# Transposing cross-attention probabilities and half of a merged sum on VectorE instead of TensorE, in a three-branch decoder layer

## The chip, the cores and the metric

The kernel runs on one core of a Trainium2 chip. The metric is the device time of one execution in microseconds (us). Times of a profiled execution are counted from the start of its span, which is the time from its first to its last instruction.

## The reference

One pre-norm layer on 256 tokens of 1024 channels, everything in float32. The input projection feeds three branches, whose outputs are projected, gated, summed and projected once more:

```python
h = rms_norm(x, norm_g)
(qa, ka, va, ga, ub, vb, gb, qc, gc, ma, mb, mc) = split_cols(h @ w_in, IN_SPLITS)
out_a = moba_attention(rope(qa), rope(ka), va) * silu(ga)      # 6 heads x 128, causal over 256 tokens
out_b = gmlp_spatial_gate(ub, vb, ...) * silu(gb)              # 6 groups x 128 channels
mk, mv = split(rms_norm(mem, mem_norm_g) @ w_mem_kv, 2)        # 256 memory tokens
p = softmax(qc @ mk.T * 128 ** -0.5)                           # 4 heads x 128, 256 x 256 each
out_c = (p @ mv) * silu(gc)
y = sigmoid(ma) * (out_a @ w_a) + sigmoid(mb) * (out_b @ w_b) + sigmoid(mc) * (out_c @ w_c)
return rms_norm(x + y @ w_out, final_norm_g)
```

## The kernel before

All weights stream once from HBM through SyncE's DMA queue, in pieces of 1 MB into a ring of three buffers (`raw`). A piece holds two **chunks** of 128 x 1024 numbers. There are 106 chunks, here counted from 0: the input projection is chunks 0 to 81 (the memory's values are 50 to 53), the branch projections are 82 to 89 for the first 512 output channels (half 0) and 90 to 97 for the others (half 1), and the output projection is 98 to 105. Within a half the order is branch a (three chunks), b (three), c (two).

Each product is made in three passes of a rounded format (fp32r): a number is split into `hi`, its rounded copy, and `lo`, the rest, and TensorE adds hi x hi, hi x lo and lo x hi. For a chunk of weights ScalarE makes `hi` (`split_hi`, L179) and then VectorE makes `lo` (`split_lo`, L183). Four chunks have room for the split, and the split of chunk c + 3 is put out while chunk c is multiplied (`LEAD` = 3, `SPL` = 4). A chunk with tokens in the stationary operand takes 12 matmuls of 512 columns (L329 to L331), and those with features there take eight of 512 and eight of 256 columns (L420).

All other work (rope, softmax, transposes, gates) is cut into units with a set cost, and a small planner (`Units`) puts them between the chunks: it keeps a clock for each engine and puts a unit out once its inputs are ready by that clock, or once it is due. What comes out is a fixed order on each engine; every engine works strictly in its order.

The places the change touches:

- For a cross head, `c_scores`, `c_max`, `softmax_exp` and `softmax_norm` give the probabilities `p` (tokens on partitions). `c_pT` turns them with four TensorE transposes of 128 x 128 against an identity (`transpose4`, L549) into a PSUM bank, ScalarE copies the rounded part (`pth`, L717), VectorE takes the rest (`ptl`, L337), and `c_pv` multiplies with the values.
- At the end of a half, the last of six gated sums (L855, L857) leaves y with tokens on partitions in the tile `sig[half]`. `y_units` turns it, in two units of four TensorE transposes each, and splits it (L192, L193) for the output projection: half 0 is needed from chunk 98 on, half 1 from chunk 102 on.
- `rms_bcast` (L277) spreads the row scales of x and of the memory over all partitions with two float32 matmuls of a matrix of ones and a diagonal matrix (`dg`, L271).
- `xk`, the token-major x, is loaded once at the start (L229), squared for the first norm, and kept in its slot (`xr`) to the end, where it is the residual.

Of the kernel before, what the change touches and what calls it, by code (L numbers as in the profile page):

```python
# [24 lines left out]
F32 = mybir.dt.float32  # L25
F32R = mybir.dt.float32r
BF16 = mybir.dt.bfloat16
AF = mybir.ActivationFunctionType
OP = mybir.AluOpType
# [3 lines left out]
D = 1024  # L33
S = 256
KD = D // 128
HA, GB, HC = 6, 6, 4
# [28 lines left out]
PE, DVE, ACT, POOL = range(4)  # L65
# [59 lines left out]
def tile_hybrid_layer(ctx: ExitStack, tc: tile.TileContext, xw, memT, mem, x, fin_g, ln_g, w, w_sp, b_sp, rope, out):  # L125
    nc = tc.nc
    ctx.enter_context(tc.manual_schedule())
    const = ctx.enter_context(tc.tile_pool(name="const", bufs=1))
    act = ctx.enter_context(tc.tile_pool(name="act", bufs=1))
    wts = ctx.enter_context(tc.tile_pool(name="wts", bufs=1))  # L130
    work = ctx.enter_context(tc.tile_pool(name="work", bufs=2))
    psum = ctx.enter_context(tc.tile_pool(name="psum", bufs=1, space=PSUM))

    V = {}

    def slot_tile(name, shape, tag, dt=F32):
        V[name] = act.tile(shape, dt, name=name, tag=tag)
        return V[name]

    def pair(name, tag, n):  # L140

        t = slot_tile(name, [128, n, 2, S], tag, F32R)
        V[name + "h"], V[name + "l"] = t[:, :, 0, :], t[:, :, 1, :]
        return V[name + "h"], V[name + "l"]

    def bank():
        return psum.tile([128, 512], F32, name="aux", tag="aux", bufs=4)
# [4 lines left out]
    def tsl(t):  # L152
        return slice(t * 128, (t + 1) * 128)

    def hsl(h):
        return slice(h * 128, (h + 1) * 128)
# [12 lines left out]
    def load(j):  # L169
        raw_alloc(j)  # L170
        load_part(j, 0, PIECE)
# [30 lines left out]
    def st_k(k, a, b):  # L202
        o = (NG if k < 4 else 0) + (k % 4) * XW
        return st[k // 4][:, o + a:o + b]
# [20 lines left out]
    load_part(2, 0, CH)  # L225
    load_part(2, CH, PIECE)
    load(3)
    V["xk"] = act.tile([128, 2, D], F32, name="xk", tag="xr")
    nc.sync.dma_start(V["xk"], x)  # L229

    warm = work.tile([128, 512], BF16, name="warm", tag="p", bufs=3)
    nc.vector.memset(warm, 0.0)
    ones = const.tile([128, 128], F32, name="ones")
    nc.vector.memset(ones, 1.0)
    eps = const.tile([128, 1], F32, name="eps")
    nc.vector.memset(eps, EPS)
    ident = const.tile([128, 128], F32, name="ident")
# [18 lines left out]
    bc = {}  # L256
# [9 lines left out]
            (DVE, 0.2, lambda: nc.vector.reciprocal(dst, rt))  # L266

    def rms_diag(r, name):
        bc["d" + name] = work.tile([128, 2, 128], F32, name="dg", tag="jt", bufs=3)
        for t in range(2):  # L270
            nc.vector.tensor_scalar(bc["d" + name][:, t, :], ident, r[:, t:t + 1], None, op0=OP.mult)  # L271

    def rms_bcast(name):

        bc["p" + name] = bank()
        for t in range(2):
            nc.tensor.matmul(bc["p" + name][:, tsl(t)], ones, bc["d" + name][:, t, :], start=True, stop=True)  # L277

    def rms_out(name):
        bc[name] = work.tile([128, S], F32, name="bc", tag="ssq", bufs=2)  # L280
        nc.scalar.activation(bc[name], bc["p" + name][:, 0:S], AF.Copy)  # L281

    def rms_all(name, r):
        return (DVE, 0.6, lambda: rms_diag(r, name)), (PE, 0.22, lambda: rms_bcast(name)), \
            (ACT, 0.4, lambda: rms_out(name))

    def gain_hi(src, g, dh):
# [7 lines left out]
    for k in range(KD):  # L295
        c, a, g = k // 2, (k % 2) * 512, gain[:, k:k + 1]
# [6 lines left out]
        gain_lo(x_k(k), g, hh[:, k, :], hl[:, k, :])  # L303
        nc.vector.tensor_tensor(lo[c][:, a:a + 512], st_k(k, S, XW), hi[c][:, a:a + 512].bitcast(F32), OP.subtract)
    nc.vector.tensor_copy(gains, gain)


    chunks = []
# [8 lines left out]
    n_br = len(chunks)  # L317
# [7 lines left out]
    U = Units(4.5, 2.5, 0.8)  # L325
    now = [0]
# [9 lines left out]
    def sub_lo(dl, p, dh):  # L336
        nc.vector.tensor_tensor(dl, p, dh.bitcast(F32), OP.subtract)  # L337
# [5 lines left out]
    sig = {}  # L343
# [155 lines left out]
    for k in range(KD):  # L499
        U.add(f"nm{k}", POOL, 1.05, lambda k=k: nc.gpsimd.tensor_tensor(x_k(k), x_k(k), bc["x"], OP.mult),  # L500
              after=["xrms"], due=7)
    for k in range(KD):
        U.add(f"nxh{k}", ACT, 0.42, lambda k=k: gain_hi(x_k(k), gain[:, k:k + 1], V["nh"][:, k, :]),
              after=[f"nm{k}", "nxa"], due=8 + k // 2)
        U.add(f"nxl{k}", DVE, 0.5, lambda k=k: gain_lo(x_k(k), gain[:, k:k + 1], V["nh"][:, k, :], V["nl"][:, k, :]),
              after=[f"nxh{k}"], due=8 + k // 2)
# [17 lines left out]
    for t in range(2):  # L524
        U.add(f"msq{t}", ACT, 1.25, lambda t=t: row_squares(V[f"mm{t}"], ssm[:, t:t + 1], V[f"mm{t}"]),
              after=["load_mem"])
# [15 lines left out]
    def rope_b(h):  # L542
        q = V["qk"][0:32, h]
        nc.vector.tensor_tensor(q, q, trig[:, 0, None, :].to_broadcast([32, 2, S]), OP.mult)
        nc.vector.tensor_tensor(q, q, ST["r", h], OP.add)

    def transpose4(p, blocks):
        for j, src in enumerate(blocks):
            nc.tensor.transpose(p[:, hsl(j)], src, ident)  # L549

    ST = {}
# [62 lines left out]
    def p_lo(kind, h, n):  # L614
        ps, pth, ptl = ST[kind + "T", h]
        sub_lo(ptl[:, 0:n], ps[:, 0:n], pth[:, 0:n])
# [23 lines left out]
    def back(stage, n):  # L640

        n -= 3 if stage == "p" else 2
        return [] if n < 0 else [f"a{stage}{n}" if n < HA else f"c{stage}{n - HA}"]
# [31 lines left out]
    for h in range(HA):  # L675
        if h == 2:
# [3 lines left out]
                after=[f"q{h}", f"k{h}", "consts"] + back("v", h) + ([f"as{h - 2}.0"] if h > 1 else []))  # L680
# [3 lines left out]
                after=[f"as{h}"])  # L684
        U.chain(f"ap{h}", (PE, 0.33, lambda h=h: a_pT(h)), (ACT, 0.72, lambda h=h: a_pT_out(h)),
                after=[f"an{h}"] + back("v", h))
# [20 lines left out]
        nc.vector.tensor_reduce(mx, ps.rearrange("p (t k) -> p t k", t=2), axis=AX.X, op=OP.max)  # L707
        ST["cm", h] = (softmax_max(mx), (ps[:, 0:256], ps[:, 256:512]))

    def c_pT(h):  # L710
        p = ST["c", h][0]
        ST["cp", h] = bank()
        transpose4(ST["cp", h], [p[:, hsl(j)] for j in (0, 2, 1, 3)])

    def c_pT_out(h):
        ps = ST["cp", h]
        nc.scalar.activation(p_tiles("c", h, ps), ps, AF.Copy)  # L717

    def c_pv(h):
# [12 lines left out]
    for h in range(HC):  # L732
        U.chain(f"cs{h}", (PE, 0.72, lambda h=h: c_scores(h)), (DVE, 0.9, lambda h=h: c_max(h)),
                (ACT, 1.15, lambda h=h: softmax_exp("c", h)),
                after=[f"qcl{h | 1}", f"mkl{h | 1}", "sqrts"] + back("p", HA + h))
        U.chain(f"cn{h}", (DVE, 0.2, lambda h=h: softmax_sum("c", h)), (ACT, 0.85, lambda h=h: softmax_norm("c", h)),
                after=[f"cs{h}"])
        U.chain(f"cp{h}", (PE, 0.44, lambda h=h: c_pT(h)), (ACT, 0.62, lambda h=h: c_pT_out(h)),
                after=[f"cn{h}"] + back("v", HA + h))
        U.chain(f"cv{h}", (DVE, 0.68, lambda h=h: p_lo("c", h, 512)), (PE, 0.72, lambda h=h: c_pv(h)),  # L740
                (ACT, 0.4, lambda h=h: c_out(h)), after=[f"cp{h}", "mvl0", "mvl1"])

    U.add("exps", None, 0, lambda: None, after=[f"as{h}" for h in range(HA)] + [f"cs{h}" for h in range(HC)])
    for name, n in (("gc", HC), ("ga", HA)):
        U.add(name + "s", ACT, n * 0.25, lambda name=name: nc.scalar.activation(V[name], V[name], AF.Silu),
              after=["exps"] + [f"{name}{i}" for i in range(n)])
# [21 lines left out]
    def gate_unit(src, g):  # L768
        nc.gpsimd.tensor_tensor(src, src, g, OP.mult)

    def two_split(name, views, after):
        def hi_part():
            src, dh, _ = views()
            nc.scalar.activation(dh, src, AF.Copy)

        def lo_part():
            src, dh, dl = views()
            nc.vector.tensor_tensor(dl, src, dh.bitcast(F32), OP.subtract)

        U.chain(name, (ACT, 0.6, hi_part), (DVE, 0.68, lo_part), after=after)  # L780

    def alloc(*specs):
        def fn():
# [1 line left out]
                slot_tile(*s)  # L785
        return fn

    U.add("oaTa", None, 0, lambda: pair("a", "x2", HA), after=["mv.0"])
    for i in range(3):
        hs = slice(2 * i, 2 * i + 2)  # L790
        U.add(f"ga_{i}", POOL, 1.6, lambda hs=hs: gate_unit(V["qk"][:, hs, 0, :], V["ga"][:, hs, :]),
              after=[f"av{2 * i}", f"av{2 * i + 1}", "gas"])
        two_split(f"oaT{i}", lambda hs=hs: (V["qk"][:, hs, 0, :], V["ah"][:, hs, :], V["al"][:, hs, :]),
                  [f"ga_{i}", "oaTa"])
    U.add("ocTa", None, 0, alloc(("och", [128, HC, S], "och", F32R), ("ocl", [128, HC, S], "ocl", F32R)),
          after=[f"cs{h}" for h in range(HC)])
    for i in range(3):
        U.chain(f"mix{i}", (PE, 0.82, lambda i=i: mix_unit(i)), (DVE, 0.85, lambda i=i: mix_bias(i)),
                after=["lna0", "lna1", f"cp{HC - 1}"])
    for i in range(3):  # L800
# [4 lines left out]
            after=[f"mix{i}", f"gbs{i}"])  # L805
    U.add("obTa", None, 0, alloc(("obh", [128, GB, S], "vb", F32R), ("obl", [128, GB, S], "v0", F32R)),
          after=["mix0", "mix1", "mix2"])
# [4 lines left out]
    for i in range(2):  # L812
        hs = slice(2 * i, 2 * i + 2)
        U.add(f"gc_{i}", POOL, 1.6, lambda hs=hs: gate_unit(V["oc"][:, hs, :], V["gc"][:, hs, :]),
              after=[f"cv{2 * i}", f"cv{2 * i + 1}", "gcs"])
# [7 lines left out]
    def y_units(half, i, after):  # L823

        k = slice(4 * half + 2 * i, 4 * half + 2 * i + 2)

        def turn():
            ST["y", half, i] = bank()
            transpose4(ST["y", half, i], [sig[half][:, t, hsl(2 * i + a)] for a in range(2) for t in range(2)])

            split2(ST["y", half, i].rearrange("p (k s) -> p k s", k=2), V["yh"][:, k, :], V["yl"][:, k, :])
            U.run(DVE, 0.7, U.run(ACT, 0.62, U.t[PE]))

        U.add(f"yt{half}{i}", PE, 0.44, turn, after=after)
# [72 lines left out]

    for c in range(n_br + 4):
        now[0] = c
        s = c + LEAD  # L910
        U.slot(c, False)
        if s > 3:
            split(s)
            U.end[f"s{s}"] = U.run(DVE, 1.23, U.run(ACT, 1.05, max(U.end.get(f"c{s - SPL}", 0), 9.0 + 1.45 * s)))
        if s % 2 == 1 and 3 < s // 2 + 2 < n_pieces:
            load(s // 2 + 2)
        kind = chunks[c][0]
        U.end[f"c{c}"] = U.run(PE, 2.78 if kind == "fea" else 2.73, U.end.get(f"s{c}", 0.0))
        if kind == "tok":
            mm_tok(c)  # L920
        elif kind == "fea":
            mm_fea(c)
        elif kind == "br":
            mm_br(c)
        else:
            mm_out(c, 0)
            for a, b in (((0, 256), (256, 512)) if chunks[c][1] else ((0, 512),)):
                mm_out(c, 1, a, b)
        U.slot(c, True)
# [106 lines left out]
```

## Time and profile before

| what | value |
|---|---|
| median of 3 runs | 327.78 us (327.61 to 327.97) |
| the profiled execution's own time | 328.44 us |
| its span | 326.4 us |
| TensorE (PE), matmuls | busy 317.9 us, 97% of the span |
| VectorE (DVE) | busy 232.2 us, 71% |
| ScalarE (ACT) | busy 201.1 us, 62% |
| GpSimd (POOL) | busy 41.3 us, 13% |
| DMA engines | 192 GB/s read on average over the span |

The profiled execution is 0.66 us longer than the median, and its span is 2.04 us shorter than its own time. Matmuls overlap, so one matmul's duration is longer than what it adds to TensorE's time; the chain of work that ended last shows what each adds.

### The profile page before, as it was taken

The numbers are of one execution on the slowest core, as the hardware profiler recorded it, in microseconds if no ns is written. First come the engines' busy times: TensorE is split into PE (matmuls) and PEld (weight loads), VectorE is DVE, ScalarE is ACT, GpSimd is POOL, SyncE is SP. The second block draws the span as 40 slices with busy tenths as digits, with TensorE's granted clock in tenths as the row PEclk, the third lists the DMA queues.
The fourth block names the chain that finished last, engine by engine and source line by source line (L and its number), as shares of the span: only waits on it lengthen the run. The fifth ranks groups of instructions, "written<-read, shape, count | busy, mean of one in ns | idle before, by whom it ended". The sixth has DMA issues, their size and how long they took to land.

```text
span 326.4 us, 4417 instructions
## 1 busy us (share of the span) xinstructions
PE 317.9 (97%) x1663; PEld 271.4 (83%) x1663; DVE 232.2 (71%) x355; ACT 201.1 (62%) x342; POOL 41.3 (13%) x39
## 2 busy tenths in 40 slices
PE   7999999999999999999999999999999999999992
PEld 4888888888888888888888889888888888888881
DVE  4968956986998778878856388785444559768452
ACT  4779787557755765786493987575654633433532
POOL 0007430000000000220000146840000000000022
PEclk9999999999999999999999999999999999999997
DMA  7999595555345446336434275455456464453002
GB/s 284 393 424 399 201 385 194 195 159 229 129 170 203 147 136 251 130 130 241 147 129 152 108 257 172 153 163 226 156 230 228 160 228 158 155 233 129 2 16 113
DMA packets 10724, 62.87 MB, mean 193 GB/s; under 512 B 1200, under 2 KB 1584, under 8 KB 4176
## 3 DMA queue, kind: packets, MB, share of 16 engines
q1 hardware_dynamic: 10416, 62.08, 52.3%
q10 hardware_dynamic: 288, 0.52, 0.4%
q8 instruction: 13, 0.21, 0.3%
q14 instruction: 7, 0.06, 0.0%
HBM read 61.55 MB, written 1.05 MB: 192 GB/s over the span
## 4 chain that ended last, share of the span: by engine, by line
PE 95%; DMA 2%; DVE 1%; ACT 1%; issue 0%; SPq 0%; DVEq 0%
PE acc L420 36%; PE acc L331 13%; PE acc L330 13%; PE acc L329 13%; PE aux L329 5%; PE aux L330 4%; PE aux L331 4%; PE acc L360 3%; PE aux L549 2%; DMA st<-in_xw_dram 2%; PE aux L758 1%; PE aux L596 0%; PE aux L635 0%; ACT jk L881 0%; PE aux L277 0%; DVE xk L879 0%
## 5 line engine op out<-in xcount | busy, mean ns | idle before, releaser
L183 DVE TENSOR_TENSOR lo<-raw,hi 128x1024 fp32r<-128x1024 f32 x102 | 129.2, 1268 | 63.4 <-ACT hi L179 63.0
L179 ACT ACTIVATE hi<-raw 128x1024 fp32r<-128x1024 f32 x102 | 107.8, 1058 | 49.1 <-PE acc L331 36.5
L420 PE MATMUL acc<-n,hi 128*128 128x512 f32 x304 | 79.7, 395 | 0.0
L420 PEld LDWEIGHTS acc<-n,hi 128*128 128x128 f32 x304 | 54.7, 189 | 9.2
L420 PEld LDWEIGHTS acc<-n,lo 128*128 128x128 f32 x304 | 41.5, 190 | 3.0
L420 PE MATMUL acc<-n,lo 128*128 128x256 f32 x304 | 42.4, 282 | 0.0
L329 PE MATMUL acc<-hi,n 128*128 128x512 f32 x80 | 31.2, 391 | 0.0
L331 PE MATMUL acc<-hi,n 128*128 128x512 f32 x80 | 31.1, 389 | 0.0
L330 PE MATMUL acc<-lo,n 128*128 128x512 f32 x80 | 31.1, 389 | 0.0
L331 PEld LDWEIGHTS acc<-hi,n 128*128 128x128 f32 x80 | 15.0, 188 | 3.1
L330 PEld LDWEIGHTS acc<-lo,n 128*128 128x128 f32 x80 | 15.0, 188 | 3.0
L329 PEld LDWEIGHTS acc<-hi,n 128*128 128x128 f32 x80 | 15.0, 188 | 3.0
L885 POOL TENSOR_TENSOR xk<-xk,fing 128x512 f32<-128x512 f32 (+1 forms) x4 | 4.0, 1013 | 100.9 <-ACT jk L881 100.9
L695 POOL TENSOR_TENSOR vb<-vb,lng 128x768 f32<-128x768 f32 x2 | 3.7, 1848 | 95.7 <-DVE vb L692 89.8
L424 ACT ACTIVATE jt<-acc 128x256 f32<-128x256 f32 x14 | 5.4, 383 | 11.6 <-PE acc L420 11.5
L500 POOL TENSOR_TENSOR st<-st,bc 128x256 f32<-128x256 f32 x8 | 8.8, 1141 | 24.8 <-ACT bc L281 24.8
L424 ACT ACTIVATE qk<-acc 128x256 f32<-128x256 f32 x12 | 4.6, 383 | 10.5 <-PE acc L420 10.4
L360 PE MATMUL acc<-hi,h 128*128 128x512 f32 (+1 forms) x34 | 9.4, 406 | 0.8 <-ACT hi L300 0.8
L329 PE MATMUL acc<-hi,a 128*128 128x512 f32 x24 | 9.4, 393 | 0.0
L331 PE MATMUL acc<-hi,a 128*128 128x512 f32 x24 | 9.3, 389 | 0.0
L330 PE MATMUL acc<-lo,a 128*128 128x512 f32 x24 | 9.3, 389 | 0.0
L329 PE MATMUL acc<-hi,obh 128*128 128x512 f32 x24 | 9.3, 389 | 0.0
(216 smaller groups left out, 606.0 us busy)
## 6 DMA issues: line engine op xcount, KB each, us to landing
raw<-in_w_dram SPq DMA_DIRECT2D x50, 1024.0 KB, 4.8
st<-in_xw_dram SPq DMA_DIRECT2D x6, 384.0 KB, 6.5
raw<-in_w_dram SPq DMA_DIRECT2D x2, 512.0 KB, 8.9
xk<-in_x_dram SPq DMA_DIRECT2D x1, 1024.0 KB, 12.5
mt<-in_memT_dram SPq DMA_DIRECT2D x2, 512.0 KB, 9.2
mm<-in_mem_dram SPq DMA_DIRECT2D x2, 512.0 KB, 10.8
out_dram<-xk SPq DMA_DIRECT2D x2, 384.0 KB, 2.5
fing<-in_fin_g_dram SPq DMA_DIRECT2D x1, 512.0 KB, 4.0
```

Of the source, the lines that this page charges most:

```text
L179: nc.scalar.activation(hi[c][:, a:b], raw[c // 2][:, o + a:o + b], AF.Copy)
L183: nc.vector.tensor_tensor(lo[c][:, a:b], raw[c // 2][:, o + a:o + b], hi[c][:, a:b].bitcast(F32), OP.subtract)
L329: nc.tensor.matmul(p, s_hi, m_hi, start=first, stop=False)
L330: nc.tensor.matmul(p, s_hi, m_lo, start=False, stop=False)
L331: nc.tensor.matmul(p, s_lo, m_hi, start=False, stop=last)
L360: nc.tensor.matmul(acc[name, o][t][:, a:b], src[:, k, tsl(t)], wt[c][:, i * 512 + a:i * 512 + b], start=k + n == 0, stop=k == KD - 1 and n ...
L420: nc.tensor.matmul(o, wt, m, start=i == 0, stop=i == len(passes) - 1)
L424: nc.scalar.activation(dst, pa, AF.Copy)
L500: U.add(f"nm{k}", POOL, 1.05, lambda k=k: nc.gpsimd.tensor_tensor(x_k(k), x_k(k), bc["x"], OP.mult), after=["xrms"], due=7)
L549: nc.tensor.transpose(p[:, hsl(j)], src, ident)
L695: nc.gpsimd.tensor_tensor(V["vb"][:, t, :], V["vb"][:, t, :], V["lng"], OP.mult)
L885: nc.gpsimd.tensor_tensor(z, z, V["fing"][:, a:b], OP.mult)
```

## The change

Three things change.

- The four transposes of each cross head and the eight of half 0 of y leave TensorE. VectorE does them in 32 x 32 blocks: `turn_rows` issues four `transpose` instructions, each of which reads 32 partitions (a) and writes 32 partitions (b = 0 to 3); one instruction holds four blocks (32 x 4 x 32 numbers, 128 columns). A head takes 16 instructions, half 0 of y takes 32, which makes 96 in all. The result lies in SBUF (`ct`, `yt`) and not in PSUM. Half 1 of y stays with TensorE.
- `ct` takes the slot of `xk`; so x is loaded at the start for the norm, and a second time before chunk 90 for the residual.
- `rms_bcast` becomes two fp32r matmuls of 256 columns, over a hi and a lo diagonal, and VectorE makes four diagonals instead of two. `ones` is written later, by a copy. Splits of attention outputs (`oaT`) get a due time.

```diff
-    V["xk"] = act.tile([128, 2, D], F32, name="xk", tag="xr")
-    nc.sync.dma_start(V["xk"], x)
+    def load_x():
+        slot_tile("xk", [128, 2, D], "xr")
+        nc.sync.dma_start(V["xk"], x)
+
+    load_x()
...
         for t in range(2):
-            nc.vector.tensor_scalar(bc["d" + name][:, t, :], ident, r[:, t:t + 1], None, op0=OP.mult)
+            nc.vector.tensor_scalar(dg[:, 0, t, :], ident, r[:, t:t + 1], None, op0=OP.mult)
+            nc.vector.scalar_tensor_tensor(dg[:, 1, t, :], ident, r[:, t:t + 1], dg[:, 0, t, :].bitcast(F32),
+                                           op0=OP.mult, op1=OP.subtract)
...
-        for t in range(2):
-            nc.tensor.matmul(bc["p" + name][:, tsl(t)], ones, bc["d" + name][:, t, :], start=True, stop=True)
+        for i in range(2):
+            nc.tensor.matmul(bc["p" + name][:, 0:S], ones, bc["d" + name][:, i].rearrange("p t s -> p (t s)"),
+                             start=i == 0, stop=i == 1)
...
+    def turn_rows(dst, src, a):
+
+        for b in range(4):
+            nc.vector.transpose(dst(slice(32 * b, 32 * b + 32), slice(32 * a, 32 * a + 32)),
+                                src(slice(32 * a, 32 * a + 32), slice(32 * b, 32 * b + 32)))
...
-    def c_pT(h):
-        p = ST["c", h][0]
-        ST["cp", h] = bank()
-        transpose4(ST["cp", h], [p[:, hsl(j)] for j in (0, 2, 1, 3)])
+    def c_pT(h, a):
+        if h == 0 and a == 0:
+            slot_tile("ct", [128, HC, 512], "xr")
+        p = ST["c", h][0].rearrange("p (t m s) -> p m t s", t=2, m=2)
+        pt = V["ct"][:, h, :].rearrange("p (m t s) -> p m t s", t=2, m=2)
+        turn_rows(lambda r, s: pt[r, :, :, s], lambda r, s: p[r, :, :, s], a)
...
-        U.chain(f"cp{h}", (PE, 0.44, lambda h=h: c_pT(h)), (ACT, 0.62, lambda h=h: c_pT_out(h)),
-                after=[f"cn{h}"] + back("v", HA + h))
+        U.chain(f"cp{h}", *[(DVE, 0.9, lambda h=h, a=a: c_pT(h, a)) for a in range(4)],
+                (ACT, 0.62, lambda h=h: c_pT_out(h)), after=[f"cn{h}"] + back("v", HA + h))
...
+        if half == 0:
+
+            if i == 0:
+                slot_tile("yt", [128, 4, S], "gc")
+            src = sig[0][:, :, 256 * i:256 * i + 256].rearrange("p t (k s) -> p k t s", k=2)
+            yt = V["yt"][:, 2 * i:2 * i + 2, :]
+            dst = yt.rearrange("p k (t s) -> p k t s", t=2)
+            U.chain(f"yt0{i}", *[(DVE, 0.9, lambda a=a: turn_rows(
+                lambda r, s: dst[r, :, :, s], lambda r, s: src[r, :, :, s], a)) for a in range(4)],
+                (ACT, 0.62, lambda: nc.scalar.activation(V["yh"][:, k, :], yt, AF.Copy)),
+                (DVE, 0.7, lambda: sub_lo(V["yl"][:, k, :], yt, V["yh"][:, k, :])),
+                after=after, due=[now[0] + 2 * i + d for d in (1, 1, 2, 2, 3, 4)])
+            return
...
     for c in range(n_br + 4):
         now[0] = c
+        if c == n_br - 8:
+
+            load_x()
```

The order on VectorE at the end of half 0, before. The first four rows are the gated sums of branch c, whose last completes y (`sigs_642`). The `lo` rows are the splits of chunks 93, 94 and then 95, with the split of the transposed y between them, followed by two products of branch a of half 1 and the splits of chunks 96 to 98.

```order
L855 TENSOR_TENSOR sigs_2285<-acc,sigs_2285 128x512
L857 TENSOR_TENSOR sigs_642<-sigs_642,sigs_2285 128x512
L855 TENSOR_TENSOR sigs_2285<-acc,sigs_2285 128x512
L857 TENSOR_TENSOR sigs_642<-sigs_642,sigs_2285 128x512
L183 TENSOR_TENSOR lo<-raw,hi 128x1024 x2
L193 TENSOR_TENSOR y<-aux,y 128x2x256 x2
L183 TENSOR_TENSOR lo<-raw,hi 128x1024
L855 TENSOR_TENSOR sigs_1922<-acc,sigs_1922 128x512 x2
L183 TENSOR_TENSOR lo<-raw,hi 128x1024 x3
```

The same place on VectorE with the change, where y is `sigs_646`; the single `lo` rows are chunks 93, 94 and 95, and the first of `x2` is chunk 96.

```order
L887 TENSOR_TENSOR sigs_646<-sigs_646,sigs_2249 128x512
L557 STREAM_TRANSPOSE yt<-sigs_646 32x4x32 x8
L183 TENSOR_TENSOR lo<-raw,hi 128x1024
L557 STREAM_TRANSPOSE yt<-sigs_646 32x4x32 x8
L183 TENSOR_TENSOR lo<-raw,hi 128x1024
L557 STREAM_TRANSPOSE yt<-sigs_646 32x4x32 x8
L183 TENSOR_TENSOR lo<-raw,hi 128x1024
L885 TENSOR_TENSOR sigs_1918<-acc,sigs_1918 128x512 x2
L344 TENSOR_TENSOR y<-yt,y 128x2x256
L557 STREAM_TRANSPOSE yt<-sigs_646 32x4x32 x8
L183 TENSOR_TENSOR lo<-raw,hi 128x1024 x2
```

All 32 transposes of y now stand ahead of the `lo` of chunk 96, in groups of eight, and each `lo` waits behind the groups in front of it.

The order on VectorE at the cross heads 0 and 1, before: the maxima of scores (`mx`, `nm`), the splits of the values (`mvl`) and the rest of the probabilities (`ptl`) between the `lo` of the chunks around 55 to 61.

```order
L572 RECIPROCAL rc<-sm 128x2
L183 TENSOR_TENSOR lo<-raw,hi 128x1024
L334 SCALAR_TENSOR_TENSOR mvl<-acc,rstm,cx 128x512 x2
L183 TENSOR_TENSOR lo<-raw,hi 128x1024 x2
L337 TENSOR_TENSOR ptl<-aux,pth 128x512 x2
L572 RECIPROCAL rc<-sm 128x2
L707 TENSOR_REDUCE mx<-aux 128x2
L556 TENSOR_SCALAR nm<-mx 128x2
L183 TENSOR_TENSOR lo<-raw,hi 128x1024 x3
```

The same place with the change; the rows begin behind the `lo` of chunk 55, and the six `lo` are chunks 56 to 61.

```order
L557 STREAM_TRANSPOSE ct<-p 32x4x32 x16
L183 TENSOR_TENSOR lo<-raw,hi 128x1024
L341 SCALAR_TENSOR_TENSOR mvl<-acc,rstm,cx 128x512
L183 TENSOR_TENSOR lo<-raw,hi 128x1024
L341 SCALAR_TENSOR_TENSOR mvl<-acc,rstm,cx 128x512
L344 TENSOR_TENSOR ptl<-ct,pth 128x512
L183 TENSOR_TENSOR lo<-raw,hi 128x1024
L557 STREAM_TRANSPOSE ct<-p 32x4x32 x8
L183 TENSOR_TENSOR lo<-raw,hi 128x1024
L557 STREAM_TRANSPOSE ct<-p 32x4x32 x8
L720 TENSOR_REDUCE mx<-aux 128x2
L569 TENSOR_SCALAR nm<-mx 128x2
```

Behind these rows stand the `lo` of chunk 60, one more pair of `mx` and `nm`, and the `lo` of chunk 61. Heads 0 and 1 put 32 transposes among six splits; heads 2 and 3 come later, with 32 more among the splits of chunks 69 to 76, where the planner puts four or eight into a slot.

## Rows read from the trace of the kernel before

**Rows 1.** The page: TensorE's busy time, and the chain that ended last, by engine.

```profile
PE 317.9 (97%) x1663; PEld 271.4 (83%) x1663; DVE 232.2 (71%) x355; ACT 201.1 (62%) x342; POOL 41.3 (13%) x39
...
PE 95%; DMA 2%; DVE 1%; ACT 1%; issue 0%; SPq 0%; DVEq 0%
```

**Rows 2.** Waits of TensorE, all: us in total, times, longest.

```profile
PE aux L242 <- DVE warm L232: 1.3, 1, 1.3
PE acc L360 <- ACT hi L300: 0.8, 1, 0.8
```

**Rows 3.** Chain that ended last, pieces: start, us added, engine, line, count.

```profile
25.23 0.44 PE aux L277 x4
...
181.57 0.44 PE aux L549 x4
...
196.10 0.12 PE aux L330
...
279.42 0.23 PE acc L331
279.65 0.87 PE aux L549 x8
```

**Rows 4.** Timeline: start, us; split of chunk 96, and its second matmul.

```profile
283.30 1.06 ACT L179 ACTIVATE hi<-raw 128x1024 fp32r<-128x1024 f32 x1 [1.14 <-PE acc L331]
...
284.54 1.22 DVE L183 TENSOR_TENSOR lo<-raw,hi 128x1024 fp32r<-128x1024 f32 x1
...
291.49 0.39 PE L330 MATMUL acc<-lo,och 128*128 128x512 f32 x1
```

**Rows 5.** VectorE in stages: stretch, length, busy us (instructions), PE clock, DMA.

```profile
150.00:177.00 27.00, 20.18 (x32) 1.00 0.50 184
...
272.00:296.00 24.00, 18.11 (x22) 1.00 0.50 178
```

**Rows 6.** Groups of VectorE instructions by shape: busy us, mean ns, idle before.

```profile
L183 DVE TENSOR_TENSOR lo<-raw,hi 128x1024 fp32r<-128x1024 f32 x102 | 129.2, 1268 | 63.4 <-ACT hi L179 63.0
...
L537 DVE STREAM_SHUFFLE rs<-qk 32x512 f32<-32x512 f32 x6 | 4.3, 725 | 0.0
...
L337 DVE TENSOR_TENSOR ptl<-aux,pth 128x512 fp32r<-128x512 f32 x4 | 2.7, 684 | 0.9 <-ACT pth L717 0.9
L707 DVE TENSOR_REDUCE mx<-aux 128x2 f32<-128x512 f32 x4 | 2.7, 681 | 1.2 <-PE aux L331 1.2
...
L337 DVE TENSOR_TENSOR ptl<-aux,pth 128x256 fp32r<-128x256 f32 x6 | 2.5, 419 | 0.1
...
L556 DVE TENSOR_SCALAR nm<-mx 128x2 f32<-128x2 f32 x10 | 1.7, 169 | 0.3
...
L334 DVE SCALAR_TENSOR_TENSOR mvl<-acc,rstm,cx 128x512 fp32r<-128x512 f32 x2 | 1.4, 748 | 0.0
```

**Rows 7.** VectorE at L271: two instructions, ns min/median/max.

```profile
L271 DVE TENSOR_SCALAR dg<-ident,rstd x2: 283/285/287, 22.9 to 23.1; 128x128 f32<-128x128 f32 x2
```

**Rows 8.** Timeline of VectorE: both diagonals, then the end of half 0.

```profile
22.85 0.48 DVE L271 TENSOR_SCALAR dg<-ident,rstd 128x128 f32<-128x128 f32 x2
...
275.81 0.69 DVE L857 TENSOR_TENSOR sigs<-sigs,sigs 128x512 f32<-128x512 f32 x1
...
280.76 1.29 DVE L193 TENSOR_TENSOR y<-aux,y 128x512 fp32r<-128x512 f32 x2 [1.47 <-ACT y L192]
...
283.34 1.28 DVE L855 TENSOR_TENSOR sigs<-acc,sigs 128x512 f32<-128x512 f32 x2
```

**Rows 9.** DMA to landing (us), an issue, and the `hi` of chunk 94.

```profile
raw<-in_w_dram SPq DMA_DIRECT2D x50, 1024.0 KB, 4.8
...
xk<-in_x_dram SPq DMA_DIRECT2D x1, 1024.0 KB, 12.5
...
265.71 0.33 SPq L167 DMA_DIRECT2D raw<-in_w_dram  x1
...
276.97 1.06 ACT L179 ACTIVATE hi<-raw 128x1024 fp32r<-128x1024 f32 x1 [1.66 <-PE acc L331]
```

More of the change, by code (lines that the diff above doesn't have):

```diff
@@ L227, in tile_hybrid_layer @@
     load(3)
-    V["xk"] = act.tile([128, 2, D], F32, name="xk", tag="xr")
-    nc.sync.dma_start(V["xk"], x)
+    def load_x():
+        slot_tile("xk", [128, 2, D], "xr")
+        nc.sync.dma_start(V["xk"], x)
+    load_x()
     warm = work.tile([128, 512], BF16, name="warm", tag="p", bufs=3)
     nc.vector.memset(warm, 0.0)
-    ones = const.tile([128, 128], F32, name="ones")
-    nc.vector.memset(ones, 1.0)
+    ones = const.tile([128, 128], F32R, name="ones")
     eps = const.tile([128, 1], F32, name="eps")
@@ L268, in rms_diag @@
     def rms_diag(r, name):
-        bc["d" + name] = work.tile([128, 2, 128], F32, name="dg", tag="jt", bufs=3)
+        bc["d" + name] = dg = work.tile([128, 2, 2, 128], F32R, name="dg", tag="jt", bufs=3)
         for t in range(2):
-            nc.vector.tensor_scalar(bc["d" + name][:, t, :], ident, r[:, t:t + 1], None, op0=OP.mult)
+            nc.vector.tensor_scalar(dg[:, 0, t, :], ident, r[:, t:t + 1], None, op0=OP.mult)
+            nc.vector.scalar_tensor_tensor(dg[:, 1, t, :], ident, r[:, t:t + 1], dg[:, 0, t, :].bitcast(F32),
+                                           op0=OP.mult, op1=OP.subtract)
     def rms_bcast(name):
         bc["p" + name] = bank()
-        for t in range(2):
-            nc.tensor.matmul(bc["p" + name][:, tsl(t)], ones, bc["d" + name][:, t, :], start=True, stop=True)
+        for i in range(2):
+            nc.tensor.matmul(bc["p" + name][:, 0:S], ones, bc["d" + name][:, i].rearrange("p t s -> p (t s)"),
+                             start=i == 0, stop=i == 1)
     def rms_out(name):
@@ L283, in rms_all @@
     def rms_all(name, r):
-        return (DVE, 0.6, lambda: rms_diag(r, name)), (PE, 0.22, lambda: rms_bcast(name)), \
+        return (DVE, 1.2, lambda: rms_diag(r, name)), (PE, 0.24, lambda: rms_bcast(name)), \
             (ACT, 0.4, lambda: rms_out(name))
@@ L305, in tile_hybrid_layer @@
     nc.vector.tensor_copy(gains, gain)
+    nc.vector.tensor_copy(ones, nc.const_aps.tensor(1.0, (128, 128), F32))
     chunks = []
@@ L708, in c_max @@
         ST["cm", h] = (softmax_max(mx), (ps[:, 0:256], ps[:, 256:512]))
-    def c_pT(h):
-        p = ST["c", h][0]
-        ST["cp", h] = bank()
-        transpose4(ST["cp", h], [p[:, hsl(j)] for j in (0, 2, 1, 3)])
+    def c_pT(h, a):
[4 more added lines that the diff above has]
+        turn_rows(lambda r, s: pt[r, :, :, s], lambda r, s: p[r, :, :, s], a)
     def c_pT_out(h):
-        ps = ST["cp", h]
+        ps = V["ct"][:, h, :]
         nc.scalar.activation(p_tiles("c", h, ps), ps, AF.Copy)
@@ L769, in gate_unit, with two_split @@
         nc.gpsimd.tensor_tensor(src, src, g, OP.mult)
-    def two_split(name, views, after):
+    def two_split(name, views, after, due=10 ** 6):
         def hi_part():
@@ L778, in lo_part @@
             nc.vector.tensor_tensor(dl, src, dh.bitcast(F32), OP.subtract)
-        U.chain(name, (ACT, 0.6, hi_part), (DVE, 0.68, lo_part), after=after)
+        U.chain(name, (ACT, 0.6, hi_part), (DVE, 0.68, lo_part), after=after, due=due)
     def alloc(*specs):
@@ L786, in alloc @@
         return fn
+    sig2 = chunks.index(("tok", "sig", 1024, 6))
     U.add("oaTa", None, 0, lambda: pair("a", "x2", HA), after=["mv.0"])
@@ L793, in tile_hybrid_layer @@
         two_split(f"oaT{i}", lambda hs=hs: (V["qk"][:, hs, 0, :], V["ah"][:, hs, :], V["al"][:, hs, :]),
-                  [f"ga_{i}", "oaTa"])
+                  [f"ga_{i}", "oaTa"], due=sig2 - 2)
     U.add("ocTa", None, 0, alloc(("och", [128, HC, S], "och", F32R), ("ocl", [128, HC, S], "ocl", F32R)),
```

## The prediction

> **What bounds the kernel now.** I read the page first: TensorE is busy for 97% of the span, and the chain that ended last runs through it for 95% [rows 1]. Next the waits of TensorE: 1.3 and 0.8 us, both at the start [rows 2]. So TensorE works through a fixed list without a gap, and the time is the length of that list plus a short head and tail. A change helps by what it takes off the list, and hurts by any wait it puts in. What each item adds is read from the chain's pieces, since one matmul's duration overlaps the next: a matmul of 512 columns adds 0.23 us and one of 256 columns 0.12 us, so a chunk of twelve long ones takes 2.7 us [rows 3].
>
> Then the question is how far the other engines are ahead. In the branch projection, chunk 96 is the example: ScalarE starts its `hi` at 283.30, VectorE ends its `lo` at 284.54 + 1.22 = 285.76, and TensorE first reads the `lo` at 291.49 [rows 4]. The lead is 5.7 us. It can't grow, because only four chunks have room; it is what a burst on VectorE may use up before TensorE waits. VectorE idles 6.8 of 27 us where the cross heads stand and 5.9 of 24 us at the end of half 0 [rows 5].
>
> **What leaves TensorE.** Four transposes of a head add 0.44 us, the eight of half 0 add 0.87 us, and two float32 matmuls with `ones` 0.44 us (shown as four passes) [rows 3]. Heads: 4 x 0.44 = 1.76. Half 0: 0.87. The two broadcasts become two fp32r matmuls of 256 columns each: 2 x (0.44 - 2 x 0.12) = 0.40. Together 3.03 us. None of this is covered by anything, since TensorE has no gap.
>
> **What one transpose costs VectorE.** No row shows this operation, and the result hangs on the distance from the start of one to the start of the next; call it tau. For the duration of 128 columns, go down from larger shapes: 256 and 512 columns take 419 and 684 ns, 1.035 ns a column [rows 6], so a plain pass takes 419 - 128 x 1.035 = 286 ns. The two diagonals of 128 columns took 285 [rows 7]. The nearest relative is the shuffle, which moves data across partitions: 725 ns for 512 columns, so 725 - 384 x 1.035 = 328 ns [rows 6]. Now the distance: both diagonals together took 0.48 us, so the second began 0.195 us after the first, 0.09 before its end [rows 7, 8]; two gated products of 0.69 took 1.28, an overlap of 0.10 [rows 8]. Independent instructions overlap by 0.09. The transposes of one group are independent, so tau lies between 0.195 and 0.328 - 0.09 = 0.24. I take 0.24, by the shuffle. Should they not overlap, tau is 0.286 to 0.328.
>
> **The end of half 0, where it decides.** Up to y the order is the same; the last gated sum ends at 275.81 + 0.69 = 276.50 [rows 8]. From there to the end of the `lo` of chunk 96 VectorE has four `lo` (4 x 1.22 [rows 4] = 4.88), two products (1.28 [rows 8]), one split of y (0.68 [rows 6]) and 32 transposes: it ends at 276.50 + 6.84 + 32 tau = 283.34 + 32 tau. TensorE wants it at 291.49 less the 0.87 of transposes that no longer stand ahead, 290.62. So it waits 32 tau - 7.28 us, from tau = 0.228 on. At 0.24 that is 0.40 us. Behind it the slack is larger: chunk 97 has its `lo` next on VectorE (1.22) while chunk 96 runs 2.7 us. ScalarE's copies of `yt` stand ahead of the `hi` of chunks 95 and 97 and follow the same transposes, so they come out in step.
>
> **The cross heads.** Between the `lo` of chunks 55 and 61 VectorE has six `lo` (7.3), two `mvl` (1.5), one `ptl` (0.68), two maxima with their scaling (1.7) [rows 6] and 32 transposes: 11.2 + 32 tau. TensorE has six chunks (16.4) and three products of six short matmuls (2.2) [rows 3]: 18.6 us. At 0.24 VectorE falls behind by 0.3 us, at 0.328 by 3.1, both within 5.7. Heads 2 and 3 spread as many over eight chunks. I put no wait here.
>
> **What I cost at nothing.** The diagonals grow from two to four instructions, some 0.6 us more by their row; they are done at 23.33 + 0.6, before TensorE comes at 25.23 [rows 3, 8]. The later copy of `ones` is one pass of 0.29 us in the first stage, where TensorE waits for no VectorE work on the way [rows 2]; without cover it costs that much. ScalarE's copies now read SBUF instead of PSUM, the same columns. The second load of x goes out right behind the piece of chunks 94 and 95, issued at 265.71; alone a piece lands in 4.8 us, and x took 12.5 in the crowded start [rows 9]. Even at 12.5 the piece lands at 278.2, 1.2 after its first use now at 276.97, and chunk 94 itself runs only two chunks before 96, after 284. Half 1's transposes move one chunk back: from transposes to the end of the split took 279.65 to 280.76 + 1.29 = 282.05, 2.4 us [rows 3, 8], against 0.87 and a chunk of 2.7. The due time of `oaT` moves splits that are needed some 40 us later.
>
> **Sum.** -3.03 + 0.40 = -2.63 us. On the span that is 326.4 to 323.8, on the profiled execution's own time 328.44 to 325.8. The median of the runs before lies 0.66 below that execution, so I predict 325.1 us for the median.
>
> **Rivals.**
>
> *Each transpose waits for the one before to end.* Then tau is 0.286 to 0.328, the wait of chunk 96 is 1.87 to 3.22, and the change is -1.2 to +0.2 us: 326.6 to 328.0. For it: each instruction writes another group of 32 partitions than the last. Against it: all overlaps I can read are of instructions that start at partition 0, so the rows neither show nor exclude it. [...]
>
> *Slower: the block must fill before anything comes out.* A transpose of 32 columns can give its first result only behind its last input column, which adds 32 x 1.035 = 33 ns to the shuffle's 328: 0.36. Without overlap the wait is 4.24 us, +1.2 us, 329.0 us. It ends on the slow side from tau = 0.343 on, where the wait passes 3.03 + 0.66. For it speaks that the shuffle, the same kind of move, already costs 42 ns more than a plain pass; against it, that fill can hide in the fixed part of some 154 ns.
>
> *The heads wait too.* The product of head 3 stands two chunks ahead of the chunk whose `lo` follows its `ptl` on VectorE, so it waits once the lead there falls below about 3.8 us. With the 3.1 us loss worked out above that would be 1.2 us: 324.75 + 1.2 = 326.0 if half 0 went free. Against it: the 32 transposes there are spread wider, and at tau = 0.24 the lead stays above 5.
>
> *It does not do what it says* is excluded for the removal: the program's list for TensorE lacks those transposes.
>
> **Chances.** Overlapping transposes 0.50 (324.7 to 325.5); each waiting for the last 0.30; fill and slow 0.12; heads late 0.08. Faster or slower is told apart from no change at 0.2%, 0.66 us. Of the second case 0.12 falls below 327.1, 0.16 within, 0.02 above; of the last 0.03, 0.04 and 0.01. Sums: faster 0.65, same 0.20, slower 0.15. The range runs from 324.3 (tau of 0.195 and no wait gives 324.75; 0.4 for the sizes of TensorE's terms) to 328.0, the end of the second case; it leaves out the slow one and a little below.
>
> **What would show it.** In the changed trace: transposes of 0.29 to 0.33 us, and a group of eight in about 2 us if they overlap, 2.3 to 2.6 if not; no VectorE-caused wait of TensorE at the heads; one wait at the first matmuls of chunk 96 for its `lo`, 0.4 us if I am right, 2 to 3 if the first rival is; L277's successor adding 0.24 us a time; ScalarE never waiting for the weights around the second load of x. The prediction is wrong if tau is above 0.30, or if TensorE waits at a place other than chunk 96.

## The result, and the profile after

The changed kernel takes 330.03 us (median of 6 runs, 329.26 to 331.25) against 327.82 us for the kernel before on the same chip: a ratio of 1.0068, 95% interval 1.0058 to 1.0078. It is slower, and outside the range. The profiled execution took 329.26 us, with a span of 327.5. Its page, to compare with [rows 1]:

```profile
PE 315.7 (96%) x1635; PEld 268.8 (82%) x1635; DVE 263.6 (80%) x455; ACT 201.9 (62%) x342; POOL 40.3 (12%) x39
...
PE 90%; DVE 7%; ACT 1%; issue 1%; DVEq 0%
```

TensorE has less to do, as forecast, but VectorE is now 7% of the chain that ended last. TensorE's waits, to compare with [rows 2] (us in total, times, longest):

```profile
PE acc L337 <- DVE lo L183: 2.6, 1, 2.6
PE aux L562 <- DVE y L193: 1.4, 1, 1.4
PE aux L244 <- DVE eps L238: 1.3, 1, 1.3
```

The last is the start, as before. The other two are new. Here is the first, on VectorE's timeline at the end of half 0 (start, us, line, count), and the matmul of TensorE that ends it; they answer to [rows 4] and [rows 8]:

```profile
273.12 0.69 DVE L887 TENSOR_TENSOR sigs<-sigs,sigs 128x512 f32<-128x512 f32 x1
273.85 2.51 DVE L557 STREAM_TRANSPOSE yt<-sigs 32x128 f32<-32x128 f32 x8
276.39 1.22 DVE L183 TENSOR_TENSOR lo<-raw,hi 128x1024 fp32r<-128x1024 f32 x1
277.65 2.52 DVE L557 STREAM_TRANSPOSE yt<-sigs 32x128 f32<-32x128 f32 x8
280.20 1.23 DVE L183 TENSOR_TENSOR lo<-raw,hi 128x1024 fp32r<-128x1024 f32 x1
281.35 2.51 DVE L557 STREAM_TRANSPOSE yt<-sigs 32x128 f32<-32x128 f32 x8
283.88 1.23 DVE L183 TENSOR_TENSOR lo<-raw,hi 128x1024 fp32r<-128x1024 f32 x1
...
286.92 2.53 DVE L557 STREAM_TRANSPOSE yt<-sigs 32x128 f32<-32x128 f32 x8
289.48 1.23 DVE L183 TENSOR_TENSOR lo<-raw,hi 128x1024 fp32r<-128x1024 f32 x1
```

```profile
290.76 0.50 PE L337 MATMUL acc<-lo,och 128*128 128x512 f32 x1 [2.58 <-DVE lo L183]
```

VectorE works without a gap from 273.85 to 290.71, and the `lo` of chunk 96 comes out at 290.71, 17 us after y. By shape, the transposes are

```profile
L557 DVE STREAM_TRANSPOSE ct<-p 32x128 f32<-32x128 f32 x64 | 19.4, 302 | 0.9
...
L557 DVE STREAM_TRANSPOSE yt<-sigs 32x128 f32<-32x128 f32 x32 | 9.7, 303 | 0.5
```

so one lasts 0.303 us, and eight in 2.51 us means that they start (2.51 - 0.303) / 7 = 0.315 us apart: each begins 0.01 us after the one before has ended. The second wait stands in half 1's transposes, behind chunk 100; pieces of the chain (start, us added):

```profile
304.52 0.45 PE aux L562 x4
304.97 0.02 issue
304.99 0.61 ACT y L192
305.60 0.02 issue
305.62 0.70 DVE y L193
306.32 0.04 issue
306.37 0.66 PE aux L562 x4
```

TensorE turned four blocks, and went on only when ScalarE (0.61 us) and VectorE (0.70) had split them.

Since matmuls overlap (a matmul of 0.39 us starts 0.23 after the one before, [rows 3] and [rows 4]), what a wait adds is read from starts and not from the idle time. The first matmul of chunk 96 before, then the same one after, and the matmuls on both sides of half 1's transposes after:

```profile
291.26 0.39 PE L329 MATMUL acc<-hi,och 128*128 128x512 f32 x1
```

```profile
287.79 0.39 PE L336 MATMUL acc<-hi,och 128*128 128x512 f32 x1
...
304.24 0.28 PE L338 MATMUL aux<-hi,y 128*128 128x256 f32 x1
...
306.37 0.66 PE L562 MATMUL aux<-ident,sigs 128*128 128x128 f32 x4 [1.41 <-DVE y L193]
306.78 0.48 PE L336 MATMUL acc<-hi,y 128*128 128x512 f32 x1
```

In chunk 96 the second matmul starts 290.76 - 287.79 = 2.97 us after the first, where it was 0.23 before [rows 4]: 2.74 us added. Around the transposes pass 306.78 - 304.24 = 2.54 us, of which a matmul's 0.12 and eight transposes' 0.87 would have passed without a wait: 1.55 us added. The sum for this execution is -3.03 + 2.74 + 1.55 = +1.26 us. Its span, 327.5 us, is 1.1 us above that of the profiled execution before (326.4), and 1.6 above the median span of the other runs of that kernel (325.9), so some 0.3 us are not accounted for. Of the six runs three have a mean granted clock of 0.995 and took 329.26 to 329.56 us, and three have 0.989 to 0.991 and took 330.51 to 331.25; the profiled one is of the first three, and what the others show on top is found below.

### The profile page after: what moved, and what is told of

Same layout as the page of the kernel before. It is cut to its first block, busy times and chain, and to the rows that moved or that the text cites. A ratio compares the mean times of both kernels' runs of the same rounds, so it can differ in the third digit from the quotient of the medians.

```text
span 327.5 us, 4479 instructions
## 1 busy us (share of the span) xinstructions
PE 315.7 (96%) x1635; PEld 268.8 (82%) x1635; DVE 263.6 (80%) x455; ACT 201.9 (62%) x342; POOL 40.3 (12%) x39
## 4 chain that ended last, share of the span: by engine, by line
PE 90%; DVE 7%; ACT 1%; issue 1%; DVEq 0%
PE acc L427 36%; PE acc L337 11%; PE acc L338 11%; PE acc L336 11%; PE aux L337 4%; PE aux L336 4%; PE aux L338 4%; PE acc L367 4%; DVE yt L557 3%; DVE lo L183 2%; PE aux L244 1%; PE aux L562 1%; PE aux L773 1%; DVE sigs L885 1%; DVE sigs L887 0%
## 5 line engine op out<-in xcount | busy, mean ns | idle before, releaser
L557 DVE STREAM_TRANSPOSE ct<-p 32x128 f32<-32x128 f32 x64 | 19.4, 302 | 0.9
L708 POOL TENSOR_TENSOR vb<-vb,lng 128x768 f32<-128x768 f32 x2 | 4.5, 2268 | 104.7 <-ACT p L592 93.5
L784 POOL TENSOR_TENSOR qk<-qk,ga 128x512 f32<-128x512 f32 x3 | 6.1, 2078 | 34.8 <-ACT ga L760 34.8
L557 DVE STREAM_TRANSPOSE yt<-sigs 32x128 f32<-32x128 f32 x32 | 9.7, 303 | 0.5
L337 PE MATMUL acc<-lo,obh 128*128 128x512 f32 x24 | 9.4, 393 | 0.0
```

The source lines that it names most:

```text
L337: nc.tensor.matmul(p, s_hi, m_lo, start=False, stop=False)
L557: nc.vector.transpose(dst(slice(32 * b, 32 * b + 32), slice(32 * a, 32 * a + 32)), src(slice(32 * a, 32 * a + 32), slice(32 * b, 32 * b + ...
L708: nc.gpsimd.tensor_tensor(V["vb"][:, t, :], V["vb"][:, t, :], V["lng"], OP.mult)
```

## The experiments

Theory A: everything that is lost is lost through the transposes of y; the heads and the broadcasts gain what they should. Theory D: the second wait is for a PSUM bank. Theory F: a transpose waits for the one before because the two use different groups of 32 partitions. The rivals stand in the expectations. The median of the kernel before was 327.97 us beside heads_only, y_only, early_half1 and merged_y, and 327.96 beside the other four.

**heads_only**: half 0 of y back on TensorE.

```diff
-        if half == 0:
+        if half == 2:
```

> Half 0 of y goes back to TensorE; the cross heads' transposes stay on VectorE, as do the second load of x and the broadcasts in fp32r. Theory A (the loss sits in the transposes of y alone): TensorE saves 1.76 us at the heads and 0.40 at the broadcasts and waits nowhere behind the start, so about 325.6 us. Rival B (any transposes on VectorE starve the splits of the weights, at the heads too, or the second load of x costs): no gain, 327.5 us or more, with a TensorE wait near the heads or for a DMA.

325.40 us, ratio 0.9921 (0.9909 to 0.9932). The only wait of TensorE is at the start:

```profile
PE aux L244 <- DVE eps L238: 1.3, 1, 1.3
```

The heads have the same slow transposes, sixteen in 5.04 us, and TensorE does not wait for them:

```profile
162.46 5.04 DVE L557 STREAM_TRANSPOSE ct<-p 32x128 f32<-32x128 f32 x16
167.53 1.23 DVE L183 TENSOR_TENSOR lo<-raw,hi 128x1024 fp32r<-128x1024 f32 x1
```

Theory A stands, rival B falls: 64 transposes of the 96 are harmless where the lead is refilled between them.

**y_only**: `c_pT` and its chain as in the kernel before, half 0 of y on VectorE.

```diff
+    def c_pT(h):
+        p = ST["c", h][0]
+        ST["cp", h] = bank()
+        transpose4(ST["cp", h], [p[:, hsl(j)] for j in (0, 2, 1, 3)])
```

> The cross heads go back to TensorE; half 0 of y stays on VectorE. Theory A: TensorE saves 0.87 + 0.40 and gets both waits seen with the whole change, 2.6 us before the lo of chunk 96 and 1.4 us in half 1's transposes, so about 330.5 us, up to 1.5 more where the clock falls in the wait. Rival B: below 328, since only a third of the transposes are left.

332.22 us, ratio 1.0130 (1.0117 to 1.0143), with the same two waits:

```profile
PE acc L337 <- DVE lo L183: 2.6, 1, 2.6
PE aux L562 <- DVE y L193: 1.4, 1, 1.4
```

So the waits need only the 32 transposes of y. The time is 1.7 us above the 330.5 expected, a little more than the 1.5 that was allowed for a fall of the clock, and the stages show where it went (stretch, length, busy us of PE, PEld, DVE, ACT and POOL with instructions, PE clock, DMA):

```profile
290.00:291.00 1.00, 0.00 (x0) 0.00 (x0) 0.96 (x4) 0.00 (x0) 0.00 (x0) 1.00 0.76 320
...
293.00:294.00 1.00, 1.00 (x5) 0.81 (x4) 1.00 (x2) 1.00 (x2) 0.00 (x0) 0.71 0.00 0
294.00:295.00 1.00, 1.00 (x4) 0.81 (x3) 1.00 (x2) 0.56 (x1) 0.00 (x0) 0.50 0.47 66
295.00:296.00 1.00, 1.00 (x4) 0.71 (x4) 1.00 (x2) 0.00 (x0) 0.00 (x0) 0.50 0.71 115
296.00:297.00 1.00, 1.00 (x4) 0.81 (x3) 0.96 (x3) 0.36 (x1) 0.00 (x0) 0.58 1.00 418
297.00:298.00 1.00, 1.00 (x6) 0.78 (x6) 0.96 (x2) 0.70 (x1) 0.00 (x0) 1.00 0.93 393
```

TensorE stood idle to 292.37. A microsecond after it began again, the granted clock fell from 1.00 to 0.50, and stayed low for some 3 us. Matmuls of chunk 96 that had started 0.24 us apart (at 292.71 and 292.95) now started 0.43 apart (at 294.26 and 294.69). By the clock of the four rows that is 0.29 + 0.50 + 0.50 + 0.42 = 1.7 us of work lost.

**early_half1**: the whole change, with half 1's transposes due behind chunk 99.

```diff
-        U.add(f"yt{half}{i}", PE, 0.44, turn, after=after)
+        U.add(f"yt{half}{i}", PE, 0.44, turn, after=after, due=99 if half else 10 ** 6)
```

> The whole change, with half 1's TensorE transposes put back behind chunk 99 instead of chunk 100. Theory D (the second wait, 1.4 us, is for a PSUM bank: behind chunk 100 three of the four aux banks hold sums of the output projection, so the second group of four waits until the first is split): the wait inside the transposes goes, at most some 0.3 us for the last gated sum remains, and the time falls by 1.1 to 1.4 us against the whole change, to about 328.8. Rival E (VectorE is simply late): the wait of 1.4 us moves to chunk 99 and the time stays.

329.12 us (12 runs), ratio 1.0023 (1.0009 to 1.0036). The second wait is gone, the first is unchanged:

```profile
PE acc L337 <- DVE lo L183: 2.6, 1, 2.6
PE aux L244 <- DVE eps L238: 1.3, 1, 1.3
PE acc L367 <- ACT hi L306: 0.4, 1, 0.4
```

Nothing took its place at chunk 99, so theory D holds and rival E falls. The runs lie in two groups. Four with a mean clock of 0.997 took 327.43 to 328.07 us; eight with 0.988 to 0.992 took 328.93 to 329.45. The medians, 327.87 and 329.21, are 1.3 us apart. Each is 1.4 to 1.6 us below the median of the changed kernel's group of like clock (329.46 and 330.63), which is the 1.55 of the second wait. The profiled one is of the second group, and shows the same fall of the clock behind the wait of chunk 96:

```profile
291.00:292.00 1.00, 1.00 (x5) 0.77 (x5) 0.96 (x1) 1.00 (x3) 0.00 (x0) 0.78 0.00 0
292.00:293.00 1.00, 1.00 (x4) 0.82 (x3) 1.00 (x3) 0.90 (x1) 0.00 (x0) 0.50 0.00 0
```

**pairs_y**: the same 32 transposes of y, ordered so that two in a row use the same partitions; both splits of y behind chunk 96.

```diff
+            def turn_pairs(a):
+                for b in range(4):
+                    for j in range(2):
+                        ra, rb = slice(32 * a, 32 * a + 32), slice(32 * b, 32 * b + 32)
+                        nc.vector.transpose(dst[j][rb, :, :, ra], src[j][ra, :, :, rb])
```

> The same 32 transposes of half 0, in another order: the instructions of both halves of the channels that read the same 32 partitions and write the same 32 partitions stand next to each other. Also, both splits of y stand behind the lo of chunk 96. Theory F (an instruction waits for the one before to end when it reads or writes another group of 32 partitions than that one): every second one overlaps, a group of eight takes 4 x 0.315 + 4 x 0.22 = 2.1 to 2.2 us instead of 2.51, the wait at chunk 96 falls from 2.6 to about 0.5 us, the bank wait of 1.4 us stays, about 327.4 us. Rival G (0.315 us is what any transpose of this size takes, whatever its neighbours): a group in 2.5 us, a wait of about 2 us, 329 us.

326.64 us, ratio 0.9966 (0.9952 to 0.9979). The first group of eight, the first two of its instructions by themselves, and the waits:

```profile
273.70 2.02 DVE L854 STREAM_TRANSPOSE yt<-sigs 32x128 f32<-32x128 f32 x8
```

```profile
273.70 0.30 DVE L854 STREAM_TRANSPOSE yt<-sigs 32x128 f32<-32x128 f32 x1
273.94 0.26 DVE L854 STREAM_TRANSPOSE yt<-sigs 32x128 f32<-32x128 f32 x1
```

```profile
PE aux L562 <- DVE y L193: 1.4, 1, 1.4
PE aux L244 <- DVE eps L238: 1.3, 1, 1.3
PE acc L337 <- DVE lo L183: 0.2, 1, 0.2
```

Same instructions, same shapes, other neighbours: 2.02 us instead of 2.51. Two of a pair take 0.505 us together instead of 0.63: the second starts 0.24 us after the first, 0.06 before its end, and lasts 0.26 instead of 0.30. Theory F holds, rival G falls. Of the fall of the wait by 2.4 us some 2.0 come from the four groups (0.49 each); the rest is put down to the split of y (0.68) that was moved behind the `lo` of chunk 96 at the same time. With the wait down to 0.2 us no run shows the low clock (0.994 to 0.997), though the bank wait of 1.4 us is still there.

**swap**: four in a row write the same 32 partitions and read four different ones.

```diff
-            nc.vector.transpose(dst(slice(32 * b, 32 * b + 32), slice(32 * a, 32 * a + 32)),
-                                src(slice(32 * a, 32 * a + 32), slice(32 * b, 32 * b + 32)))
+            nc.vector.transpose(dst(slice(32 * a, 32 * a + 32), slice(32 * b, 32 * b + 32)),
+                                src(slice(32 * b, 32 * b + 32), slice(32 * a, 32 * a + 32)))
```

> The whole change with the two roles exchanged in the loop: four instructions in a row write the same 32 partitions and read four different ones. If theory F holds for reads as for writes: sixteen in 5.05 us and eight in 2.5 us, as now. If only the written partitions count: three of four overlap, eight in about 1.9 us, and the wait at chunk 96 all but goes.

A single run: 330.96 us, the same two waits, a mean clock of 0.989, and

```profile
163.00 5.05 DVE L557 STREAM_TRANSPOSE ct<-p 32x128 f32<-32x128 f32 x16
```

Sixteen that change the partitions they read take 5.05 us here, and sixteen that change those they write take 5.04 in heads_only: neither order shows an overlap.

**half_y**: 16 transposes of y on VectorE, the other unit on TensorE.

```diff
-        if half == 0:
+        if half == 0 and i == 0:
```

> Only the first half of the channels of half 0 is turned on VectorE (16 instructions), the other four transposes go back to TensorE. Theory A: 16 x 0.315 = 5.0 us ahead of the lo of chunk 96, which then is ready about 2 us early; no wait, and TensorE saves 1.76 + 0.44 + 0.40 = 2.6: 325.3 us. Rival H (the wait grows from the first transposes on, in proportion): a wait of 1.3 us at chunk 96, 327 us.

324.92 us, ratio 0.9913 (0.9899 to 0.9926); TensorE waits at the start alone. The `lo` of chunk 96 starts at 284.81 and takes 1.2 us, and TensorE first reads it at 288.34, some 2.3 us after its end. Five microseconds of transposes fit in front of it, ten do not: the wait begins where the room is used up and does not grow from the first transpose on, so rival H falls.

**rms_only**: all transposes on TensorE, with the fp32r broadcasts and the second load of x; it is heads_only and y_only in one.

> All transposes are back on TensorE; the broadcasts in fp32r and the second load of x stay. Theory A: 0.40 us saved and nothing lost, 327.5 us. Rival B: the second load of x delays a weight piece, and the time is above that of the kernel before.

327.27 us (11 runs), ratio 0.9979 (0.9971 to 0.9988): 0.7 us less, where 0.40 was worked out. The second load costs nothing that shows: TensorE's two waits, 1.3 and 0.3 us, are for VectorE and ScalarE, none for a DMA. The chain shows the 0.24 us of each broadcast that was expected:

```profile
25.03 0.24 PE aux L282 x2
```

The other 0.3 us lie outside the span. A run of the kernel before takes 2.03 to 2.16 us longer than its span, and every run of a kernel here, the changed one included, 1.66 to 1.79. By span, rms_only's median is 325.5 us against 325.9 before, which is the 0.40. What makes the 0.35 us outside the span stays open, since the profiles begin with the first instruction and end with the last.

**merged_y**: one instruction of 256 columns where there were two of 128, a quarter of them behind the `lo` of chunk 96, and half 1 as in early_half1.

```diff
+            src = sig[0].rearrange("p t (k s) -> p k t s", k=4)
+            dst = V["yt"].rearrange("p k (t s) -> p k t s", t=2)
+            U.chain("yt0", *[(DVE, 1.8, lambda a=a: turn_rows(
+                lambda r, s: dst[r, :, :, s], lambda r, s: src[r, :, :, s], a)) for a in range(4)],
...
+                after=after, due=[now[0] + d for d in (1, 2, 3, 5, 6, 6, 6, 7)])
```

> Half 0 of y is turned by 16 instructions of 256 columns instead of 32 of 128, four in each of four slots, the last four behind the lo of chunk 96; half 1's transposes go back behind chunk 99. Theory A (a start-to-start of 0.315 us, of which 0.18 is paid once per instruction): 0.45 us each, a group of four in 1.8 us, no wait of TensorE, and the whole saving of 3.03 us stays: 324.8 us. Rival C (the time goes with the number of 32 x 32 blocks): a group of four in 2.4 to 2.5 us, and the gain smaller.

324.62 us, ratio 0.9897 (0.9882 to 0.9911): faster than both kernels. By shape and in groups of four:

```profile
L557 DVE STREAM_TRANSPOSE yt<-sigs 32x256 f32<-32x256 f32 x16 | 7.0, 436 | 0.3
```

```profile
274.16 1.78 DVE L557 STREAM_TRANSPOSE yt<-sigs 32x256 f32<-32x256 f32 x4
```

They start (1.78 - 0.436) / 3 = 0.45 us apart: twice the columns for 0.13 us more. Rival C falls. Behind the first 7 us TensorE waits for nothing. This kernel changes the number of instructions, their places and half 1 at once, so it shows what the idea is worth, not which of the three counts most.

## Why the prediction was wrong

**What leaves TensorE** was right: the broadcasts add 0.24 us each, heads_only gains 2.57 us for 2.16 worked out, half_y 3.04 for 2.60, merged_y 3.35 for 3.03. The 0.3 to 0.4 us more lie outside the span: by the medians of the spans the gains are 2.2, 2.75 and 3.0. The prediction took the same gain for the span and for the time; these 0.35 us it did not have.

**What one transpose costs VectorE** is the step that failed: "The transposes of one group are independent, so tau lies between 0.195 and 0.328 - 0.09 = 0.24". The duration was right (0.303 us, between the 0.286 and 0.328 named). The overlap was not: the 0.09 was read from instructions that all start at partition 0, and carried over to instructions that each read or write another group of 32. Measured, tau is 0.315 us; pairs_y gets an overlap of 0.06 us back by the order alone, and swap shows that it makes no difference whether the reading or the writing changes (sixteen in 5.05 us, as in 5.04). That is the first rival, to which I gave 0.30.

**The end of half 0.** The formula held: 32 x 0.315 - 7.28 = 2.80 us, 2.74 measured from start to start, at the matmul that was named. Only tau was wrong.

**Half 1's transposes** were costed at nothing, and that failed as well: "Half 1's transposes move one chunk back: [...] 2.4 us [...] against 0.87 and a chunk of 2.7". I compared times and did not count PSUM banks. Of four `aux` banks the two sums of output columns 0 to 511 hold two; chunk 100 takes a third for the last 256 columns. Behind chunk 99 both units find a bank each; behind chunk 100 one is left, and the second unit waits through the split of the first: 1.41 us idle, 1.55 added. Early_half1 removes it by moving the unit alone. So even the first rival's own time (326.6 to 328.0) was too low. Both signs of being wrong that the prediction named came: tau is above 0.30, and TensorE waits at a second place.

**The clock** was in no step. A wait of 2.6 us was priced at its length; in 16 of 23 executions of kernels with that wait it cost more, by their mean clocks (0.988 to 0.992). The three runs of the changed kernel at the lower mean clock are 1.2 us slower than the other three (medians 330.63 and 329.46), the groups of early_half1 are 1.3 us apart, and the rows of y_only show 1.7 us of work lost. With 1.7 and the 0.35 outside the span the sum is -3.03 + 2.74 + 1.55 + 1.7 - 0.35 = +2.6 us, measured +2.8; without the clock it is +0.9, measured +1.6, so that 0.7 us of those three runs stay open. The median of all six, +2.2, lies between the groups and shows neither. The profiled execution alone would have hidden this.

**The cross heads and the second load of x** came out as said: no wait at the heads, none for a DMA. The other two rivals fell: no transpose costs 0.36 us, and head 3 is not late.

## What to carry to other kernels

Before work is moved to an engine that has idle time on average, set the new burst against the room in front of the next result that is due: here, by the prediction's sum, 7.28 us of transposes have room between y and the `lo` of chunk 96; 5 us fit, and 10 us cost more than they saved. Take the distance between instructions from a row with the same pattern of partitions, and where there is none, forecast with no overlap (here 0.315 us apart where 0.24 was forecast); fewer and wider instructions (256 columns in 0.45 us instead of two of 128 in 0.63), or neighbours on the same partitions (a pair in 0.505), got some of it back here. When a unit moves behind another, count who holds its PSUM banks at the new place, not only whether there is time: here that added 1.55 us. And compare runs of like clock before a sum is held against a median.

## What was not expected of the hardware

A wait of TensorE cost more than its length here. Behind the 2.6 us wait the granted clock fell from 1.00 to 0.50 for about 3 us; the traces of y_only and early_half1 show it. By their mean clocks (0.988 to 0.992 against 0.994 and more) it happened in 3 of 6 runs of the changed kernel, 8 of 12 of early_half1, all 4 of y_only and the one of swap; of the changed kernel the only trace is of a run where it did not. It did not happen in the 5 runs of pairs_y, whose longest wait in the middle was 1.4 us, nor in the 4 of half_y, which has none there. Why some executions with the same wait keep the clock stays open.
